# Pacing the bulk transfers of a fused decoder layer in counted TensorE time, and storing K and V once per pair of chunks

## The chip, the cores and the metric

The kernel runs on all eight cores of one Trainium2 chip. The metric is the device time of the slowest core in microseconds (us), as the median of several executions. Each execution lists the span and the mean granted TensorE clock of every core. The executions of this case show a second, slower state: in some of them all four cores of one die, sometimes of both, have a lower clock (0.80 to 0.96 as a mean), and the time is up to 14% longer (2957.6 us for the kernel before in the group of e13 to e16, where the median of its fast executions is 2599.1 us). Such executions were left out.

Two numbers are used side by side. The time is that of the slowest core. The mean span is the mean over the eight cores and all fast executions; it is less noisy, because the slowest of eight is a matter of luck as well as of work.

## The reference, cut to what matters

One decoder layer over 4 sequences of 8192 tokens, width 1024. It mixes a gated causal convolution and an attention with forgetting, then runs a dense gated feed-forward network.

```python
def reference(x, g_mix_pre, w_in, b_forget, conv_w, conv_b, conv_ln_g, conv_ln_b,
              w_out, g_mix_post, g_ffn_pre, w_gate, w_up, w_down, g_ffn_post):
    h = rmsnorm(x, g_mix_pre[l])
    proj = h @ w_in[l]                                       # 1024 -> 2568 columns
    a_val, a_gate, q, k, v, f_logit = jnp.split(proj, splits, axis=-1)
    u = a_val * jax.nn.sigmoid(a_gate)                       # gates
    u = causal_depthwise_conv(u, conv_w[l], conv_b[l])       # width 31, 512 channels
    conv_out = jax.nn.silu(layernorm(u, conv_ln_g[l], conv_ln_b[l]))
    ...                                                      # 8 heads of 64, causal softmax,
    attn = forgetting_attention(heads(q), heads(k), heads(v), log_f)   # logits + sum of log f
    mix = jnp.concatenate([conv_out, attn_out], axis=-1) @ w_out[l]
    x = x + rmsnorm(mix, g_mix_post[l])
    h = rmsnorm(x, g_ffn_pre[l])
    y = (jax.nn.silu(h @ w_gate[l]) * (h @ w_up[l])) @ w_down[l]       # 2816 wide
    return x + rmsnorm(y, g_ffn_post[l])
```

## The kernel before

Two cores share a sequence. Each computes K and V for all 16 chunks of 512 tokens, and queries, convolution, attention and feed-forward for its own 8 chunks (every other one). All engines follow one static order, recorded by a small scheduler when the program is built. A filler stream (first the projection stage, then the feed-forward stage) is interleaved with the attention stream by counted TensorE time: `fa[0]` is the counted time of filler matmuls so far, `fa[1]` that of attention. Counted means that the program adds 512/2400 us for 512 columns; nothing in it knows about waits. `tick()` runs deferred steps, one per so many filler groups, and `defer(tag, steps, first, every)` queues them. A buffer carries keys; a DMA or an instruction waits for whatever was recorded earlier on the same keys, including earlier readers.

Two queues carry the transfers. SP issues the ring loads of K and V that attention reads (136 KB each for K, five buffers), the loads of the feed-forward weights, and all stores. POOL issues x (four pieces of 512 KB per chunk), the windows u for the convolution (four pieces of 540 KB), and 60 conversions that read the float32 feed-forward weights and write bfloat16 copies (256 KB for one of the gate and up weights).

The parts that the change touches:

```python
    # weights of the gates, recorded before chunk 0's K and V; the "read" of hT[1] only sets its place in time
    wl("q", winQ, 0, C_Q, C_K, hT[0].keys[7:8])
    wl("g", winG, 0, 0, C_Q, hT[1].keys[7:8])
    yield from p_kv(0)
    yield from norm_fin(1)                 # writes hT[1]
    flush("h")
    load_x(2)
    ...
    # K and V, chunk i: one staging buffer for K, two for V, stores per chunk
    def st_k():
        for o in range(2):
            st("sp", k_s[:, 0:64, :].rearrange(...)[o, :, :, i * CH:(i + 1) * CH],
               kst[64 * o:64 * o + 64, :, :], kst.keys, [("k_s", i, o)], ("kst", o))
    defer("st", [st_k], 4)
    ...
    # x and u: deferred pieces
    defer("x", [lambda g=g: x_piece(nxt, g) for g in range(4)], 6, 2)
    defer("lu", [lambda s=s: ld("pool", u4, ...) for s in range(4)], 1, 3)
    ...
    # LayerNorm after the convolution: two temporaries, one step at every tick
    L, C = tmp[cb % 2], cvst[cb % 2]
    ...
    defer("ln", [fs[0][0], fs[1][0], fs[0][1], fs[1][1], fs[2][0], fs[0][2], fs[1][2],
                 fs[3][0], fs[2][1], fs[3][1], fs[2][2], fs[3][2]], 3)
    ...
    # last projection chunk: weights and activations of feed-forward block 0
    if last:
        ld("pool", wout, wout[:], wout_d)
        f_load(0)                          # conv and attention activations, 0.5 MB each, on SP
        f_loadx(0)                         # x1, 2 MB, on SP
    ...
    # the seam: first part of the feed-forward stream
    yield from conv_ln(J - 1)
    yield from A1(0, range(8))             # output projection of block 0, uses wout and the loads above
    yield from gates(J, 0, H)
    flush("ln")
    yield from A2(0)                       # norm and residual
    w_pump()
    for cb in (1, 2, 3):
        yield from gates(J, cb, H)
    yield from A3(0)
    ...
    # attention of block j starts 8 us of counted filler after its queries were queued for storing
    t0 = fa[0]
    while fa[0] < min(t0 + 8.0, p_end[0]):
        yield None
    ...
    # main loop
    for c in filler():
        fa[0] += c
        tick()
        ntick[0] += 1
        if cvt and ntick[0] > 90 and ntick[0] % 8 == 0:
            cvt_one()                      # one conversion on POOL
        ...                                # then attention steps, by a rate
```

The softmax here doesn't subtract the row's maximum and nothing guards it: scores larger than these inputs give would overflow.

## Time and profile before

The time before is 2597.2 us (median of 4 executions, 2587.4 to 2603.4). In the profiled execution the cores span 2560.4 to 2605.8 us with a mean of 2585.8 us. Core 6 was the slowest, and its page is shown first: the span, the busy time of each engine, and three of the rows of 40 slices (65 us each; tenths of busy time, of the granted clock and of the DMA engines).

```profile
span 2605.8 us, 53522 instructions; the slowest of 8 cores (2560.4 to 2605.8 us)
PE 2392.7 (92%) x19688; PEld 1216.8 (47%) x19688; DVE 993.7 (38%) x1506; ACT 1598.0 (61%) x1945; POOL 510.0 (20%) x835
PE   4887989899879978999999999999999999999996
PEclk8998989999999998999999999999999999999998
DMA  9656658596564744435544553653563564453443
```

TensorE is the limiter, but not evenly. From slice 17 on it is full. Up to about 1090 us it is not, and that is the projection stage and the seam to the feed-forward stage. The windows view of the same core gives the stages and, below, two windows of 16 us, a stall and what follows it. Columns: window, its length, busy time of PE, PEld, DVE, ACT and POOL with counts, granted clock, DMA share, GB/s.

```profile
0.00:65.00 65.00, 28.89 (x119) 9.77 (x119) 17.70 (x30) 13.43 (x21) 4.85 (x12) 0.88 0.95 180
65.00:330.00 265.00, 223.75 (x1748) 113.16 (x1749) 104.94 (x181) 137.09 (x193) 66.47 (x175) 0.91 0.62 146
330.00:600.00 270.00, 244.75 (x2296) 122.74 (x2294) 107.17 (x180) 177.41 (x220) 59.00 (x148) 0.97 0.67 148
600.00:892.00 292.00, 255.59 (x2397) 131.69 (x2396) 110.03 (x185) 182.84 (x223) 49.84 (x128) 0.95 0.62 135
1090.00:2366.00 1276.00, 1262.60 (x10711) 664.19 (x10709) 463.33 (x670) 908.35 (x1057) 241.02 (x270) 1.00 0.49 148
...
768.00:784.00 16.00, 2.82 (x21) 1.20 (x19) 1.38 (x2) 0.79 (x1) 0.00 (x0) 0.65 1.00 215
784.00:800.00 16.00, 16.00 (x155) 8.95 (x154) 3.94 (x7) 11.73 (x17) 3.38 (x15) 0.92 0.58 128
```

Between 768 and 784 us TensorE stood still for 13 us while the DMA share was 1.00; the clock in that window is 0.65 and still 0.92 in the next. What it waited for is in the view of waits, PE lines of core 6 (total us, times, longest), where `s_kr` is the K ring and `s_hT` the normalised chunk:

```profile
PE pbig L355 <- DMA s_kr_52<-k_s: 32.7, 4, 16.0
...
PE pbig L355 <- DVE s_hT_77 L438: 15.8, 4, 12.7
PE pbig L355 <- DMA s_kr_53<-k_s: 14.3, 3, 7.7
...
PE pbig L355 <- DMA s_kr_49<-k_s: 5.2, 1, 5.2
```

Two of these are seen in the chain of waits of core 6 (start, us, what). First the one long wait for `hT`, then the stall at 768 us:

```profile
30.42 33.96 DMA s_winG<-w_in
...
749.17 33.88 DMA s_kr_52<-k_s
```

At 30.42 us the load of the gate weights is issued; DVE may not write the last eighth of hT1 before it has landed, since that load is recorded as a reader of it. So part of these 34 us becomes a wait of TensorE, 12.7 us on core 6. At 749.17 us a ring load of 136 KB is issued and takes 34 us, while four pieces of x, four of u, four conversions and K and V stores are issued on core 6 (739 to 767 us; the DMA share from 739 to 784 us is 0.89); that these bytes delay it is what the experiments test.

| K-ring waits before, us per core | 0-190 us | about 205 us | 240-600 us | 600-850 us | seam, 850 us on | sum |
|---|---|---|---|---|---|---|
| before | 3.6 | 15.6 | 2.3 | 8.1 | 6.7 | 36.3 |

### The profile page before, as it was taken

What the parts mean: (1) busy time and instruction counts of PE and PEld (TensorE: products, weight loads), DVE (VectorE), ACT (ScalarE), POOL (GpSimd) and SP (SyncE); (2) the same over time, 40 slices, a digit from 0 to 9 for tenths busy, and PEclk for the clock granted to TensorE, in tenths of its full rate; (3) what the DMA queues carried; (4) which work ended last, traced back from release to release, by engine and by line L of the source; (5) the groups of instructions that cost most, each with busy time, mean ns of one, the idle gap of its engine ahead of it and who ended that gap; (6) DMA issues with size and microseconds to landing.
All of it is one profiled execution on the core that took longest, in us unless ns stands there. A gap on an engine that the chain in (4) does not pass through costs nothing.

```text
span 2605.8 us, 53522 instructions; the slowest of 8 cores (2560.4 to 2605.8 us)
## 1 busy us (share of the span) xinstructions
PE 2392.7 (92%) x19688; PEld 1216.8 (47%) x19688; DVE 993.7 (38%) x1506; ACT 1598.0 (61%) x1945; POOL 510.0 (20%) x835
## 2 busy tenths in 40 slices
PE   4887989899879978999999999999999999999996
PEld 1353434444344533455555555555555555554442
DVE  2442443434242344324424324424332342433643
ACT  2264766767566665777767767767767777773311
POOL 0141212121211122014013003102201401301401
PEclk8998989999999998999999999999999999999998
DMA  9656658596564744435544553653563564453443
GB/s 180 154 116 150 158 121 178 122 199 135 145 145 98 161 143 121 154 94 157 161 155 124 166 176 108 178 173 94 154 213 91 143 187 129 133 166 130 148 151 99
DMA packets 203468, 378.67 MB, mean 145 GB/s; under 512 B 23472, under 2 KB 117168, under 8 KB 201936
## 3 DMA queue, kind: packets, MB, share of 16 engines
q1 hardware_dynamic: 178608, 307.68, 40.6%
q0 software_dynamic: 24608, 67.56, 13.1%
q8 instruction: 166, 2.72, 0.4%
q14 instruction: 86, 0.70, 0.1%
HBM read 348.35 MB, written 68.81 MB: 160 GB/s over the span
## 4 chain that ended last, share of the span: by engine, by line
PE 72%; DMA 8%; ACT 8%; DVE 5%; issue 4%; SPq 1%; POOL 1%; DVEq 0%; ACTq 0%; POOLq 0%
PE pbig L355 72%; DMA s_kr_53<-k_s 3%; DMA s_kr_52<-k_s 2%; SPq L327 1%; DMA s_winG<-w_in 1%; ACT s_pt_61 L1004 1%; ACT s_pt_60 L1004 1%; ACT s_pt_59 L1004 1%; DMA q_s<-s_qst 1%; ACT L367 1%; DMA s_xs<-xT 1%; ACT s_sq L450 1%; POOL s_pt_61 L1009 1%; ACT s_pt_62 L1004 0%; ACT s_rstd L367 0%
## 5 line engine op out<-in xcount | busy, mean ns | idle before, releaser
L1004 ACT ACTIVATE s_pt_59<-pbig 128x1024 bf16<-128x1024 f32 x288 | 294.4, 1022 | 248.2 <-PE pbig L355 247.1
L1004 ACT ACTIVATE s_pt_60<-pbig 128x1024 bf16<-128x1024 f32 x288 | 294.3, 1022 | 145.1 <-PE pbig L355 143.5
L1004 ACT ACTIVATE s_pt_61<-pbig 128x1024 bf16<-128x1024 f32 x288 | 294.2, 1022 | 121.9 <-PE pbig L355 120.4
L1004 ACT ACTIVATE s_pt_62<-pbig 128x1024 bf16<-128x1024 f32 x224 | 228.9, 1022 | 82.8 <-PE pbig L355 80.9
L1009 POOL TENSOR_SCALAR_AFFINE_SELECT s_pt_61<-s_pt_61 128x128 bf16<-128x128 bf16 x192 | 67.5, 352 | 873.6 <-ACT s_pt_61 L1004 857.0
L844 DVE SCALAR_TENSOR_TENSOR s_sa_132<-s_th_93,pbig 128x512 f32<-128x512 f32 x88 | 60.4, 687 | 261.8 <-ACT s_th_93 L843 248.8
L844 DVE SCALAR_TENSOR_TENSOR s_sa_133<-s_th_94,pbig 128x512 f32<-128x512 f32 x88 | 60.4, 686 | 236.4 <-ACT s_th_94 L843 233.2
L392 POOL TENSOR_TENSOR s_ssA<-s_ssA,s_sqr_98 128x512 f32<-128x512 f32 x55 | 75.6, 1374 | 257.3 <-ACT s_sqr_98 L385 255.7
L355 PE MATMUL pbig<-s_h_123,s_wr_124 128*128 128x512 bf16 x464 | 121.4, 387 | 4.5 <-DVE s_h_123 L438 4.1
L392 POOL TENSOR_TENSOR s_ssA<-s_ssA,s_sqr_97 128x512 f32<-128x512 f32 x57 | 78.0, 1369 | 231.1 <-ACT s_sqr_97 L385 229.5
L355 PE MATMUL pbig<-s_h_123,s_wr_127 128*128 128x512 bf16 x480 | 122.1, 381 | 0.7 <-DVE s_sa_133 L844 0.7
L355 PE MATMUL pbig<-s_h_123,s_wr_125 128*128 128x512 bf16 x464 | 118.7, 381 | 3.3 <-DVE s_sa_133 L844 3.3
L355 PE MATMUL pbig<-s_h_123,s_wr_126 128*128 128x512 bf16 x480 | 121.2, 378 | 0.0
L355 PE MATMUL pbig<-s_h_123,s_wr_129 128*128 128x512 bf16 x464 | 117.4, 378 | 3.3 <-DVE s_sa_133 L844 1.8
L355 PE MATMUL pbig<-s_h_123,s_wr_128 128*128 128x512 bf16 x464 | 117.4, 378 | 0.0
L450 ACT ACTIVATE s_sq<-s_xs 128x512 bf16<-128x512 f32 x128 | 75.1, 625 | 50.1 <-DMA s_xs<-xT 49.8
L877 DVE COPY s_mix<-pbig 128x512 f32<-128x512 f32 x56 | 38.5, 688 | 153.1 <-PE pbig L355 153.1
L819 DVE COPY s_mix<-pbig 128x512 f32<-128x512 f32 x64 | 44.2, 691 | 105.5 <-PE pbig L355 105.5
L843 ACT ACTIVATE s_th_94<-pbig 128x512 f32<-128x512 f32 x88 | 52.2, 593 | 47.8 <-PE pbig L355 47.8
L355 PE MATMUL pbig<-s_sq,s_ones_bf 128*128 128x512 bf16 x192 | 56.2, 403 | 23.5 <-ACT s_sq L450 19.3
L355 PE MATMUL pbig<-s_u_84,s_w_82 128*32 128x512 bf16 x1024 | 70.4, 397 | 6.1 <-ACT s_th_94 L581 5.9
L843 ACT ACTIVATE s_th_93<-pbig 128x512 f32<-128x512 f32 x88 | 52.2, 594 | 36.0 <-PE pbig L355 30.9
(286 smaller groups left out, 4965.4 us busy)
## 6 DMA issues: line engine op xcount, KB each, us to landing
s_xs<-xT POOLq DMA_DIRECT2D x48, 512.0 KB, 8.2
s_u_84<-u_s POOLq DMA_DIRECT2D x32, 540.0 KB, 10.6
s_wr_126<-wg_b SPq DMA_DIRECT2D x30, 512.0 KB, 4.0
s_wr_127<-wu_b SPq DMA_DIRECT2D x30, 512.0 KB, 4.6
s_wr_124<-wg_b SPq DMA_DIRECT2D x29, 512.0 KB, 4.5
s_wr_125<-wu_b SPq DMA_DIRECT2D x29, 512.0 KB, 4.7
s_wr_128<-wg_b SPq DMA_DIRECT2D x29, 512.0 KB, 4.2
s_wr_129<-wu_b SPq DMA_DIRECT2D x29, 512.0 KB, 4.5
```

The source lines that it names most:

```text
L327: P.dma(q, lambda e: e.dma_start(out=out, in_=in_), reads=reads, writes=keys, sem=sem or buf.name)
L355: P.op("pe", lambda e: e.matmul(out, lhsT=lhsT, rhs=rhs, start=start, stop=stop, **kw), reads=reads, writes=[wkey])
L367: P.op("act", lambda e: e.activation(out=r[:, 0:ncol], in_=pb[b][:, 0:ncol], func=AF.Ln, bias=epsb[:, 0:1], scale=scale), reads=[PB(b)] + ...
L392: P.op(eng, lambda e: e.tensor_tensor(out=ss[:], in0=ss[:], in1=d[:], op=ALU.add), reads=ss.keys + d.keys, writes=ss.keys)
L450: defer("sq", [lambda k=k: P.op("act", lambda e: e.activation(out=sq[:, k, :], in_=xs[:, k, :], func=AF.Square), reads=[xs.keys[k]], write ...
L819: P.op("dve", lambda e, b=b, ob=ob: e.tensor_copy(out=mix[:, ob, :], in_=pb[b][:]), reads=[PB(b)], writes=[mix.keys[ob]])
L843: P.op("act", lambda e: e.activation(out=T[:], in_=pb[bg][:], func=AF.Tanh, scale=0.5), reads=[PB(bg)], writes=T.keys)
L844: defer("ff", [lambda: P.op("dve", lambda e: e.scalar_tensor_tensor(out=A[:], in0=T[:], scalar=1.0, in1=pb[bg][:], op0=ALU.add, op1=ALU.mult),
L877: P.op("dve", lambda e: e.tensor_copy(out=mix[:, ob, :], in_=pb[b][:]), reads=[PB(b)], writes=[mix.keys[ob]])
L1004: P.op("act", lambda e: e.activation(out=p[:], in_=pbig[:, 2 * s:2 * s + 2, :], func=AF.Exp), reads=[PB(2 * s), PB(2 * s + 1)], writes=p.keys)
L1009: sel = lambda e, ap: e.affine_select(out=ap, in_=ap, pattern=[[1, 128]], base=0, channel_multiplier=-1, compare_op=ALU.is_ge, fill=0.0)
```

## The change

Its intent: no two bulk transfers should leave POOL at once. x, u and the conversions pass through one list, one at a time, at least 3 us of counted TensorE time apart (conversions at least 10.5). K and V are staged for two chunks and stored once per pair, in rows twice as long. That needs room, which comes from sharing buffers; the LayerNorm gets by with one temporary and a slower pace, the gate weights load later, and the seam is put in another order. The core of the diff, with cuts marked:

```diff
-    kst = BP("kst", [128, 4, CH], BF16, parts=4)
+    kst = BP("kst", [128, 4, 2, CH], BF16, parts=8)
-    vst = [BP("vst0", [128, NH, 4, 65], BF16)]
...
+    vst = OV("vst", [128, NH, 8, 65], BF16, sqr[0])
...
+    bulk = []
+    def bulk_flush(tag):
+        for t in [t for t in bulk if t[0] == tag]:
+            bulk.remove(t)
+            t[1]()
...
-            defer("x", [lambda g=g: x_piece(nxt, g) for g in range(4)], 6, 2)
+            defer("x", [lambda g=g: bulk.append(("x", lambda: x_piece(nxt, g))) for g in range(4)], 6, 2)
...
-            L, C = tmp[cb % 2], cvst[cb % 2]
+            L, C = m2, cvst[cb % 2]
...
-        defer("ln", [fs[0][0], fs[1][0], fs[0][1], fs[1][1], fs[2][0], ...], 3)
+        defer("ln", [fs[0][0], fs[0][1], fs[1][0], fs[0][2], fs[1][1], ...], 3, 1 if j > NOWN - 3 else 2)
...
-        wl("g", winG, 0, 0, C_Q, hT[1].keys[7:8])
         yield from p_kv(0)
         yield from norm_fin(1)
         flush("h")
         load_x(2)
+        wl("g", winG, 0, 0, C_Q, hT[1].keys[7:8])
...
-        defer("lu", [lambda s=s: ld("pool", u4, ...) for s in range(4)], 1, 3)
+        for s in range(4):
+            bulk.append(("u", lambda s=s: ld("pool", u4, ...)))
...
-                   kst[64 * o:64 * o + 64, :, :], kst.keys, [("k_s", i, o)], ("kst", o))
-        defer("st", [st_k], 4)
+                   kst[64 * o:64 * o + 64, :, :, :].rearrange("p a b t -> p a (b t)"), kst.keys, [("k_s", j, o)], ("kst", o))
+        if own:
+            defer("st", [st_k], 4)
...
+            while not cvt_done.issuperset(keys):      # in w_pump: a conversion that is needed is forced
+                cvt_one()
...
+        yield from A1(0, range(8))
         yield from conv_ln(J - 1)
-        yield from A1(0, range(8))
-        yield from gates(J, 0, H)
-        flush("ln")
         yield from A2(0)
         w_pump()
-        for cb in (1, 2, 3):
+        for cb in range(4):
             yield from gates(J, cb, H)
         yield from A3(0)
+        yield ("att", 4.0)                            # 4 us of attention
...
-        if cvt and ntick[0] > 90 and ntick[0] % 8 == 0:
+        t = fa[0] + fa[1]
+        if bulk and t >= nb[0]:
+            nb[0] = t + 3.0
+            bulk.pop(0)[1]()
+        elif cvt and t >= nb[0] and t >= nb[1]:
+            nb[0], nb[1] = t + 3.0, t + 10.5
             cvt_one()
```

## The prediction

> **What bounds the kernel now.** One static instruction order per core, with TensorE the limiter. The windows of the slowest core (core 6, 2605.8 us) show two regimes. From 1090 to 2366 us TensorE is busy 1262.6 of 1276 us at clock 1.00: nothing to gain. From 0 to 1090 us it is busy 923 us at clock 0.88 to 0.97: 167 us idle, and roughly 60 us lost to the lower clock. That is the projection stage and its seam with the feed-forward stage; the change touches only these.
>
> What TensorE waits for there (table of waits, core 6): K-ring loads 52 us in 8 waits (longest 16.0); one DVE write of hT 12.7 us; squares 19 us; exponentials, tanh and attention normalisation some 60 us in pieces of 1 to 3 us. K-ring waits are about 15 us on core 1 (2560 us), 26 on core 0, 39 and 45 on cores 2 and 3: most of the spread between cores. They coincide with DMA shares of 0.9 to 1.07 over 15 to 45 us. At 738 to 784 us x (2 MB), u (2.1 MB), five conversions and two sets of K/V stores pass together; K-ring loads then take 11 to 34 us in the chain of waits. [...]
>
> **What the change does.**
> 1. x, u and conversions leave POOL one at a time, 3 us of counted TensorE work apart, conversions 10.5. In the built order only about 38 of 60 conversions remain in the projection stage; the rest move into the first feed-forward block, where the DMA share is about 0.5. For the 738 us burst I count about 7 MB for 10.
> 2. K/V per pair: 16 K stores for 32, 8 V stores for 16, rows twice as long, same bytes. Nothing is ready later: readiness was per pair already. With 1: three quarters of the K-ring waits go: -35 us on the slowest cores, -10 on the fastest.
> 3. The gate weights load after hT1 is written. Before, their load (34 us) "read" hT1's last eighth, so DVE could not write it until the load landed: -12 us (8.5 to 15 on other cores).
> 4. LayerNorm steps every 2 ticks instead of 1: same work, less bunched against exponentials: -5 us.
> 5. Seam: A1 before the LayerNorm statistics, gates undivided, 4 us of attention before the first feed-forward matmul. Waits of 4.7, 4.1, 2.5 and several of 1 to 2 us stand at 908 to 1000 us: -10 us.
> 6. Each removed long stall removes a stretch at lower clock: windows of 16 us after stalls show 0.76 to 0.92, about 3 us each: -12 us. [...]
>
> Added: no matmuls; the 1 MB V store can still hold K loads behind it.
>
> **Prediction.** 2596.5 - 76 = 2520 us; range 2485 to 2560. Faster by over 2%: 0.74; within 2%: 0.24; slower: 0.02.
>
> **What would show it.** TensorE waits on K-ring loads below 15 us on every core; no 12 us wait at 52 us, chunk 2's matmuls starting near 73 us instead of 87; DMA share rarely 1.0 from 330 to 890 us; V stores of 1040 KB landing within 20 us; clock from 65 to 890 us up from 0.91-0.97 to 0.96 or more; the part after 1090 us unchanged in length; cores within 30 us of each other.
>
> **What would make it wrong.** x, u and K/V bytes alone still fill the DMA engines; larger stores delay ring loads; the winG load competes with x(2) and returns the 12 us; small ACT-bound gaps keep the clock low.

## More of the kernel before

K-ring waits, with all buffers of the ring counted, were 52.2 us on core 6 and 21.9 us on core 1.

Before, core 6 had issued all 60 conversions when the last chunk's first K copy came.

## The result, and the profile after

The changed kernel takes 2566.4 us (median of 4 executions, 2563.2 to 2572.5), against 2597.2 us. The ratio is 0.9887, with a 95% interval of 0.9851 to 0.9924; in a later group of runs it was 0.9836 (0.9794 to 0.9877; run `e5_changed_again`, on chip 12). A ratio is the mean time of one kernel's fast runs over that of the other's of the same rounds, so it is not quite the ratio of the medians. The gain is real, 31 us, and less than 2% in the first comparison. The prediction, 2520 us with 2485 to 2560, was too low by 46 us and its range missed.

The page of the slowest core after (core 0):

```profile
span 2570.9 us, 53213 instructions; the slowest of 8 cores (2547.3 to 2570.9 us)
PE 2378.1 (92%) x19358; PEld 1219.1 (47%) x19688; DVE 993.2 (39%) x1505; ACT 1604.7 (62%) x1951; POOL 510.0 (20%) x835
PE   6887899999899779999999999999999999999895
PEclk9998999999999889999999999999999999999997
DMA  8764656467375755765635645554563563444542
```

(330 PE records are missing from this trace, 19358 against 19688, so small differences in PE busy time are not read.) The cores now lie within 24 us of each other instead of 45. The first slice is fuller (6 tenths for 4), and the dip moved (core 6 before and core 0 after, so only roughly comparable): before, slices 12 and 15 had 7 tenths, now slices 14 and 15 have (about 835 to 965 us), with a clock of 0.8 there. The stages of core 6, for comparison with the windows above:

```profile
0.00:65.00 65.00, 40.53 (x166) 14.83 (x170) 21.92 (x35) 18.03 (x29) 4.88 (x12) 0.95 0.82 164
65.00:330.00 265.00, 222.25 (x1755) 114.39 (x1784) 105.96 (x183) 140.44 (x194) 64.09 (x172) 0.92 0.62 148
330.00:600.00 270.00, 254.06 (x2441) 130.76 (x2469) 119.67 (x203) 198.94 (x247) 56.26 (x138) 0.99 0.64 146
600.00:892.00 292.00, 261.13 (x2493) 134.75 (x2526) 100.02 (x168) 186.59 (x224) 56.50 (x152) 0.95 0.68 147
1090.00:2366.00 1276.00, 1250.87 (x10339) 659.92 (x10530) 468.13 (x675) 887.04 (x1038) 246.08 (x276) 1.00 0.51 149
```

The first 65 us hold 12 us more work, the stretch from 330 us 9 us more. From 65 to 330 us nothing changed, and the clock from 600 to 892 us is 0.95 as before. The K-ring waits of core 6 in the view of waits fell from 52.2 us in eight waits to 28.1 us in five:

```profile
PE pbig L355 <- DMA s_kr_53<-k_s: 15.5, 1, 15.5
...
PE pbig L355 <- DMA s_kr_52<-k_s: 6.2, 1, 6.2
...
PE pbig L355 <- DMA s_kr_50<-k_s: 3.4, 2, 2.7
...
PE pbig L355 <- DMA s_kr_49<-k_s: 3.0, 1, 3.0
```

On core 1, the fastest before, they rose from 21.9 to 24.1 us, each time in three waits. The two longest are at the same places on every core: one at about 205 us, one at the seam. The chain of waits of core 6 shows the second one, and the 8 us windows what it costs:

```profile
842.73 35.48 DMA s_kr_53<-k_s
```

```profile
848.00:856.00 8.00, 8.00 (x111) 3.55 (x109) 1.44 (x2) 4.80 (x6) 1.37 (x5) 1.00 0.95 166
856.00:864.00 8.00, 6.96 (x110) 2.86 (x102) 2.25 (x3) 4.78 (x7) 3.01 (x10) 1.00 1.00 202
864.00:872.00 8.00, 0.00 (x0) 0.00 (x0) 0.00 (x0) 0.56 (x1) 1.12 (x2) 0.55 0.99 264
872.00:880.00 8.00, 1.32 (x3) 0.57 (x5) 0.00 (x0) 0.44 (x1) 0.00 (x0) 0.50 0.72 199
```

A ring load issued at 842.73 us lands at 878.2 us, TensorE stands from 863 to 878 us, and the clock falls to 0.50. The profile before has 0.92 in the 16 us from 784 us on, which is an estimated 2.6 us at half clock (16 times 0.08, doubled). The clock record itself has 0.50 from 864.7 to 881.8 us, where TensorE stood from 863.0 to 878.5; before, it has 0.50 until 786.6 us, 3.3 us after the stall. What that clock costs is in the timeline before: four matmuls of 512 columns took 1.91 us from 784.1 us on, at 0.50, and 1.03 us from 788.3 us on, at 1.00.

What that ring load stands behind is in the timeline, the queue of SP first and then POOL's issues, core 6 (start, us of issuing, what):

```profile
838.20 0.37 SPq L330 DMA_DIRECT2D v_s<-s_vst  x1
838.62 0.58 SPq L327 DMA_DIRECT2D s_cv<-conv_s  x1
839.25 2.24 SPq L327 DMA_DIRECT2D s_at<-attn_s  x1
841.52 0.79 SPq L327 DMA_DIRECT2D s_x_0_117<-xT  x1
...
842.73 0.44 SPq L327 DMA_DIRECT2D s_kr_53<-k_s  x1
...
844.48 16.32 SPq L327 DMA_DIRECT2D s_kr_49<-k_s  x1
```

```profile
839.26 0.59 POOL L327 DMA_DIRECT2D s_wout<-w_out  x1 [5.66 <-PE pbig L355]
839.84 0.53 POOL L430 DMA_DIRECT2D wg_b<-w_gate  x1
847.13 0.55 POOL L430 DMA_DIRECT2D wu_b<-w_up  x1 [0.22 <-issue]
864.52 0.60 POOL L430 DMA_DIRECT2D wu_b<-w_up  x1
```

Within 5 us there leave a V store (1 MB), the activations of block 0 (twice 0.5 MB), x1 (2 MB), the output weights (2 MB written) and a conversion, then the ring load, then another conversion. The next ring load after it needs 16 us to be issued at all.

To say where time went on all eight cores, stretches were cut at fixed pieces of work: the first K copy to SBUF of chunks 1, 2, 4, 8, 12, 14 and 15, the second and the last load of convolution activations in the feed-forward stage, and the end. Means over the eight cores of the profiled execution, us; the last five columns are the K-ring waits of TensorE:

| kernel | to chunk 1 | 1-2 | 2-4 | 4-8 | 8-12 | 12-14 | 14-15 | seam | steady | tail | span | 0-190 | at 205 | 240-600 | 600-850 | seam wait |
|---|---|---|---|---|---|---|---|---|---|---|---|---|---|---|---|---|
| before | 65.3 | 23.9 | 159.3 | 239.8 | 226.0 | 113.3 | 22.0 | 221.4 | 1275.4 | 239.4 | 2585.8 | 3.6 | 15.6 | 2.3 | 8.1 | 6.7 |
| changed | 53.5 | 25.7 | 151.9 | 233.7 | 218.3 | 108.0 | 24.1 | 224.2 | 1275.3 | 244.5 | 2559.3 | 1.6 | 7.7 | 0.0 | 0.0 | 15.2 |

So 11.8 us come from the start and 24.7 us from the stretches between chunks 1 and 14. The stretch into chunk 15, the seam and the tail took 10.0 us back. Half of what the tail lost is an accident of this execution: see the last section. Waits for K-ring loads fell by 11.8 us per core, not by 35: the stalls from 240 to 850 us are gone, the one at 205 us was halved, and that of the seam more than doubled.

### The profile page after: what moved, and what is told of

Same layout as the page of the kernel before. It is cut to its first block, busy times and chain, and to the rows that moved or that the text cites. A ratio compares the mean times of both kernels' runs of the same rounds, so it can differ in the third digit from the quotient of the medians.

```text
span 2570.9 us, 53213 instructions; the slowest of 8 cores (2547.3 to 2570.9 us)
## 1 busy us (share of the span) xinstructions
PE 2378.1 (92%) x19358; PEld 1219.1 (47%) x19688; DVE 993.2 (39%) x1505; ACT 1604.7 (62%) x1951; POOL 510.0 (20%) x835
## 3 DMA queue, kind: packets, MB, share of 16 engines
q1 hardware_dynamic: 165936, 307.68, 41.3%
## 4 chain that ended last, share of the span: by engine, by line
PE 77%; ACT 8%; DMA 4%; DVE 4%; issue 4%; POOL 1%; SPq 1%; DVEq 0%; ACTq 0%; POOLq 0%
PE pbig L355 77%; ACT s_pt_60 L1018 1%; ACT s_pt_61 L1018 1%; ACT s_pt_59 L1018 1%; DMA s_kr_53<-k_s 1%; SPq L327 1%; DMA k_s<-s_kst 1%; DMA q_s<-s_qst 1%; ACT s_sq L461 1%; ACT L367 1%; DMA s_xs<-xT 1%; ACT s_pt_62 L1018 1%; DMA s_kr_50<-k_s 1%; POOL s_pt_61 L1023 0%; ACT s_rstd L367 0%
## 5 line engine op out<-in xcount | busy, mean ns | idle before, releaser
L355 PE MATMUL pbig<-s_h_121,s_wr_123 128*128 128x512 bf16 x452 | 118.4, 387 | 4.1 <-DVE s_sa_131 L859 3.4
L355 PE MATMUL pbig<-s_h_121,s_wr_124 128*128 128x512 bf16 x455 | 119.5, 385 | 1.5 <-DVE s_sa_131 L859 0.2
L355 PE MATMUL pbig<-s_h_121,s_wr_125 128*128 128x512 bf16 x459 | 118.4, 381 | 1.8 <-DVE s_sa_131 L859 0.7
L355 PE MATMUL pbig<-s_h_121,s_wr_127 128*128 128x512 bf16 x435 | 111.9, 378 | 4.9 <-DVE s_sa_131 L859 1.8
L355 PE MATMUL pbig<-s_h_121,s_wr_122 128*128 128x512 bf16 x434 | 114.2, 387 | 2.0 <-issue 0.4
L355 PE MATMUL pbig<-s_h_121,s_wr_126 128*128 128x512 bf16 x448 | 114.9, 378 | 0.9
L461 ACT ACTIVATE s_sq<-s_xs 128x512 bf16<-128x512 f32 x128 | 75.0, 625 | 50.5 <-DMA s_xs<-xT 50.1
L858 ACT ACTIVATE s_th_93<-pbig 128x512 f32<-128x512 f32 x88 | 52.2, 593 | 52.6 <-PE pbig L355 52.6
L858 ACT ACTIVATE s_th_92<-pbig 128x512 f32<-128x512 f32 x88 | 52.2, 593 | 38.8 <-PE pbig L355 33.7
## 6 DMA issues: line engine op xcount, KB each, us to landing
s_u_83<-u_s POOLq DMA_DIRECT2D x32, 540.0 KB, 11.8
```

The lines of the kernel that those rows point to most:

```text
L355: P.op("pe", lambda e: e.matmul(out, lhsT=lhsT, rhs=rhs, start=start, stop=stop, **kw), reads=reads, writes=[wkey])
L461: defer("sq", [lambda k=k: P.op("act", lambda e: e.activation(out=sq[:, k, :], in_=xs[:, k, :], func=AF.Square), reads=[xs.keys[k]], write ...
L858: P.op("act", lambda e: e.activation(out=T[:], in_=pb[bg][:], func=AF.Tanh, scale=0.5), reads=[PB(bg)], writes=T.keys)
```

## The experiments

Eighteen runs were made, in five groups, each group on one chip with the kernel before. The table has, from the fast runs, the median time of the slowest core, its ratio with the 95% interval, and the mean span less that of the kernel before on the same chip. This last difference repeats within about 2 us in the one pair that tests it (runs `e6` and `e18` are the same kernel: -41.3 and -39.8). But the kernel before itself differs by 3 us between two groups on one chip (2588.5 and 2585.3 us of mean span on chip 12; 2590.9 and 2587.7 on chip 5), so less than 3 us between runs of different groups is not read as an effect.

| run | median us | ratio | mean span less before, us |
|---|---|---|---|
| e1_gate_load_alone | 2585.9 | 0.9957 (0.9910-1.0004) | -12.6 |
| e2_no_conv_in_seam | 2561.8 | 0.9848 (0.9826-0.9870) | -31.9 |
| e3_store_per_chunk | 2567.8 | 0.9871 (0.9849-0.9893) | -27.1 |
| e4_old_seam | 2565.5 | 0.9862 (0.9840-0.9884) | -26.5 |
| e5_changed_again | 2565.6 | 0.9836 (0.9794-0.9877) | -31.4 |
| e6_early_loads_and_hold | 2557.4 | 0.9808 (0.9766-0.9850) | -41.3 |
| e7_spacing_undone | 2573.2 | 0.9859 (0.9816-0.9902) | -27.0 |
| e8_spaced_all_conversions | 2573.5 | 0.9862 (0.9821-0.9904) | -23.4 |
| e9_ln_every_tick | 2595.1 | 0.9949 (0.9932-0.9966) | -4.1 |
| e10_pairs_only | 2604.8 | 0.9979 (0.9955-1.0004) | -0.3 |
| e11_spacing_only | 2596.2 | 0.9952 (0.9936-0.9969) | -2.1 |
| e12_best | 2558.4 | 0.9803 (0.9781-0.9826) | -42.9 |
| e13_old_ln_in_changed (wrong result) | 2573.0 | 0.9905 (0.9891-0.9919) | -19.3 |
| e14_pairs_only_old_ln | 2584.7 | 0.9948 (0.9920-0.9975) | -11.9 |
| e15_spacing_only_old_ln | 2574.5 | 0.9908 (0.9891-0.9925) | -17.5 |
| e16_new_ln_only | 2584.4 | 0.9950 (0.9933-0.9966) | -11.4 |
| e17_block1_later | 2544.6 | 0.9768 (0.9734-0.9801) | -51.8 |
| e18_early_loads_again | 2558.4 | 0.9817 (0.9785-0.9848) | -39.8 |

The stretches, as in the table above:

| kernel | to chunk 1 | 2-4 | 4-8 | 8-12 | 12-14 | 14-15 | seam | steady | at 205 | 240-850 | seam wait | waits for ACT |
|---|---|---|---|---|---|---|---|---|---|---|---|---|
| before | 65.3 | 159.3 | 239.8 | 226.0 | 113.3 | 22.0 | 221.4 | 1275.4 | 15.6 | 10.4 | 6.7 | 47.0 |
| e1 | 52.8 | 159.8 | 238.7 | 224.1 | 109.1 | 21.8 | 222.0 | 1275.4 | 16.6 | 6.2 | 7.3 | 45.4 |
| e2 | 52.8 | 152.9 | 233.2 | 218.3 | 107.8 | 23.0 | 218.0 | 1277.1 | 8.1 | 0.0 | 7.5 | 44.9 |
| e3 | 52.7 | 150.2 | 232.9 | 218.8 | 108.0 | 27.8 | 220.3 | 1276.3 | 7.8 | 0.3 | 12.7 | 45.4 |
| e4 | 52.8 | 152.1 | 233.6 | 218.3 | 108.0 | 23.6 | 226.5 | 1276.2 | 7.5 | 0.0 | 14.6 | 43.6 |
| e5 (changed) | 53.7 | 152.8 | 233.3 | 218.0 | 107.7 | 23.7 | 224.5 | 1275.5 | 8.7 | 0.0 | 15.3 | 45.4 |
| e6 | 53.1 | 151.8 | 232.0 | 217.3 | 107.7 | 22.9 | 215.0 | 1277.3 | 8.0 | 0.0 | 0.0 | 49.2 |
| e7 | 53.4 | 163.8 | 235.3 | 218.8 | 109.0 | 23.3 | 216.4 | 1275.2 | 16.4 | 2.3 | 6.7 | 45.5 |
| e8 | 53.7 | 151.9 | 232.3 | 217.8 | 108.1 | 25.9 | 230.0 | 1275.2 | 8.5 | 0.2 | 21.8 | 45.3 |
| e9 | 53.2 | 152.1 | 240.4 | 225.9 | 114.1 | 26.6 | 229.7 | 1275.5 | 8.2 | 0.0 | 15.5 | 60.0 |
| e13 | 53.5 | 153.0 | 235.5 | 219.5 | 108.0 | 25.8 | 226.8 | 1275.4 | 8.2 | 0.0 | 14.4 | 50.5 |
| e14 | 53.5 | 166.6 | 234.7 | 220.0 | 109.8 | 27.0 | 220.5 | 1275.6 | 17.5 | 1.2 | 6.1 | 45.1 |
| e15 | 53.4 | 152.6 | 236.8 | 219.6 | 107.6 | 26.7 | 229.5 | 1274.9 | 8.3 | 0.3 | 14.6 | 46.3 |
| e16 | 53.2 | 161.2 | 236.6 | 229.6 | 111.2 | 21.5 | 220.5 | 1275.5 | 16.4 | 13.1 | 6.7 | 43.9 |
| e18 (e6 again) | 53.5 | 151.8 | 233.4 | 218.5 | 108.2 | 22.8 | 214.8 | 1277.8 | 8.8 | 0.0 | 0.0 | 49.6 |
| e17 | 53.2 | 139.4 | 228.5 | 218.3 | 110.6 | 20.3 | 213.9 | 1286.1 | 3.9 | 0.5 | 0.0 | 54.1 |

(The stretches of e5 and e8 up to the seam are from seven cores, since a landmark was missing on the eighth. "Waits for ACT" is what TensorE waited for ACT from 30 to 1120 us. Chunks 1 to 2 took 25.5 to 27.2 us in every variant and are left out.)

The theory after the first look: the change works in the middle of the projection stage, and the delayed conversions, now in the seam, give part of it back; the rest of the seam's wait is x1 and the activations. The rivals: the new order of the seam is what costs; or the doubled V store is, by holding ring loads behind it; or the conversions do not matter, and the seam's loads alone fill the engines.

### e1: the gate weights' load alone

```diff
 # the kernel before, with one line moved
-        wl("g", winG, 0, 0, C_Q, hT[1].keys[7:8])
         ...
         load_x(2)
+        wl("g", winG, 0, 0, C_Q, hT[1].keys[7:8])
```

> The kernel before with one line moved: the gate weights load after hT1 is written. Theory: the start-up gain of 9 to 13 us seen on the changed kernel is this line's alone, so chunk 2's first K copy comes at 77 to 82 us (86 to 93 before) and the whole run is 8 to 12 us shorter than before (ratio 0.9955 to 0.997). Rival: the later load only competes with chunk 2's input or with later traffic, and less than 4 us is left at the end.

Measured: -12.6 us of mean span, chunk 1 reached at 52.8 us instead of 65.3. The stall at 205 us and that of the seam are as before. This one line is worth some 12 of the change's 31 us. One of the six executions (2619.5 us) had two cores at a clock of 0.958; without it the difference is -15.4 us. By stretches, about 2 of the 12.5 us won up to chunk 1 are lost again from chunk 1 to 2 (26.1 us instead of 23.9).

### e2: no conversions in the seam

```diff
 # the changed kernel
+        if last:
+            hold[0] = True                  # from the K of the last chunk ...
-        elif cvt and t >= nb[0] and t >= nb[1]:
-            nb[0], nb[1] = t + 3.0, t + 10.5
+        elif cvt and t >= nb[0] and t >= nb[1] and not hold[0]:
+            nb[0], nb[1] = t + 3.0, t + pace[0]
         yield ("att", 4.0)
+        hold[0], pace[0] = False, 8.0       # ... to the end of the seam
```

> The changed kernel, but no weight conversion is issued from the last chunk's K projection to the first feed-forward matmul (they follow at 8 instead of 10.5 us of counted work). Theory A: the new K-ring stall of 14.4 to 16.7 us that every core shows at about 857 to 872 us comes from conversions that the change moved there; it falls to 6 us or less, and the run is 10 to 14 us faster than the changed kernel (about 2553 us). Theory B (the doubled V and K stores hold the ring load) and theory C (w_out, x1, the two activations are a burst of their own, the old kernel only met it less exposed): the stall stays at 11 us or more and the time within 5 us of the changed kernel.

Measured: the seam's wait fell from 15.2 to 7.5 us per core, the seam from 224 to 218 us. So the few conversions in it cause about half of the wait. The end gained at most 4 to 5 us (slowest core 2561.8); by mean span, -31.9 against -31.4 (e5, another group), nothing. The steady part became 1.6 us longer. On core 6 the 24 conversions that were left went out in bunches between 935 and 1149 us, up to four within 2 us; that this made the steady part longer is likely and not shown.

### e3: stores per chunk again, spacing kept

```diff
 # the changed kernel
-                   kst[64 * o:64 * o + 64, :, :, :].rearrange("p a b t -> p a (b t)"), kst.keys, [("k_s", j, o)], ("kst", o))
-        if own:
-            defer("st", [st_k], 4)
+                   kst[64 * o:64 * o + 64, :, i % 2, :], kst.keys[i % 2::2], [("k_s", i, o)], ("kst", o))
+        defer("st", [st_k], 4)
 # and the same for V, from one half of the pair's buffer
```

> The changed kernel, but K and V are stored per chunk again, in rows half as long, from the same buffers. Theory B: the stall at 857 to 872 us shrinks by 5 us or more and nothing else gets worse: 5 to 10 us faster than the changed kernel. Rival (the long rows are what removed the K-ring stalls of chunks 11 to 15): stalls of 5 us or more come back on some cores between 600 and 830 us, and the run is 10 to 25 us slower than the changed kernel. If the even spacing of loads removed them, neither happens: within 5 us, with the stall at 12 to 16 us.

Measured: -27.1 us, against -31.4 us for the changed kernel (e5, on another chip). No stall came back between 240 and 850 us (0.3 us), the seam's wait is 12.7 us. With the spacing in place the longer stores add nothing that these runs can tell from zero: at most 4 us. With stores per chunk the seam's wait is 2.5 us shorter than in e5 (12.7 against 15.3 us), so the doubled store may be that much of it while conversions pass beside it. Without conversions there it adds nothing: e7 and e14 below have the doubled store and waits of 6.7 and 6.1 us, as before the change (6.7). The second rival falls for the most part.

### e4: the old order of the seam

```diff
 # the changed kernel, with the seam as before
+        yield from conv_ln(J - 1)
         yield from A1(0, range(8))
-        yield from conv_ln(J - 1)
+        yield from gates(J, 0, H)
+        flush("ln")
         yield from A2(0)
...
-        yield ("att", 4.0)
```

> The changed kernel with the order of the seam as before (LayerNorm statistics first, gates split, no attention ahead of the first feed-forward matmul). If the new order is worth the 10 us that I predicted, this run is 8 to 12 us slower than the changed kernel. The traces say less: from the end of the K-ring stall to the second load of conv activations the new order is 4 us shorter on core 1, so 2 to 6 us slower is what I now expect, with the stall at 860 us unchanged at 14 to 17 us.

Measured: the seam takes 226.5 us instead of 224.3, the wait in it is 14.6 us. By this stretch the new order is worth 2 to 3 us (by mean span -26.5 against -31.4 us, but in different groups), and it does not cause the stall. The first rival falls.

### e5: the changed kernel again, as a reference on the chip of the next three

> The changed kernel once more, unaltered, to have it on the same chip as the next three. Expected: ratio to before 0.985 to 0.989, mean span of the eight cores 2554 to 2558 us, one K-ring stall of 14 to 17 us at about 870 us on every core.

Measured: 2565.6 us, ratio 0.9836, and the same stretches as in the first profile within 1 us, except the tail (242.5 us instead of 244.5). Two of its six executions were slow.

### e6: block 0's activations loaded one chunk earlier, and no conversions in the seam

```diff
 # e2, with the conversions resumed at a pace of 5.5 instead of 8.0, and
         if last:
             ld("pool", wout, wout[:], wout_d)
-            f_load(0)
-            f_loadx(0)
...
+        if i == NCH - 2:                    # during chunk 14
+            f_loadx(0)
+            f_load(0)
```

> The changed kernel with no conversion in the seam (as in e2_no_conv_in_seam, resumed at 5.5 us of counted work so that none is forced later), and with x1, the conv activations and the attention output of the first own chunk loaded during chunk 14 instead of in the seam (3 MB out of the burst). Theory: the seam stall is bytes ahead of the ring load; conversions were 8 us of 15 and the remaining 5.8 to 9.7 us of e2_no_conv_in_seam fall below 3: mean span 2544 to 2548 us, ratio 0.980 to 0.983. Rival: what is left is the K and V stores of the last pair and w_out, and the stall stays at 5 us or more with a mean above 2551.

Measured: the seam's wait is 0.0 us on every core, the mean span -41.3 us, 10 us better than the changed kernel on the same chip. The windows of core 6 in the place of the stall (shown above for the changed kernel):

```profile
856.00:864.00 8.00, 7.94 (x77) 4.43 (x76) 2.00 (x5) 5.88 (x9) 2.50 (x6) 1.00 0.25 70
864.00:872.00 8.00, 7.95 (x68) 4.17 (x67) 3.34 (x6) 6.31 (x8) 3.80 (x4) 1.00 0.17 52
```

TensorE is full at clock 1.00, with a DMA share of 0.17 to 0.25 where it was 0.99. The stall is thus made of conversions (half, e2) and of the loads of x1 and the activations (the other half). The loads stood there before the change already; the conversions were put there by it.

### e7: spacing undone

```diff
 # the changed kernel: x, u and conversions leave as before
-            defer("x", [lambda g=g: bulk.append(("x", lambda: x_piece(nxt, g))) for g in range(4)], 6, 2)
+            defer("x", [lambda g=g: x_piece(nxt, g) for g in range(4)], 6, 2)
 # the same for u
-        elif cvt and t >= nb[0] and t >= nb[1]:
+        ntick[0] += 1
+        if cvt and ntick[0] > 90 and ntick[0] % 8 == 0:
```

> The changed kernel with only the bulk queue undone: x, u and conversions leave POOL as before (all conversions by 645 us of counted work); pairs, seam, LayerNorm and gate load stay changed. Theory: the bulk queue is the whole of the change beyond the gate load, so K-ring stalls of 3 to 13 us come back on most cores near 640 to 660 and 770 to 790 us, the stall at about 210 us grows to 14 to 18, the seam stall falls to 4 to 10, and the mean span is 2566 to 2573 us, as for e1_gate_load_alone. Rival: pairs, seam and LayerNorm do part of it together, mean 2560 or less.

Measured: -27.0 us, 4.4 us worse than the changed kernel on the same chip. Without spacing, the stretch from chunk 2 to 4 is 11 us longer (the wait at 205 us is back at 16.4 us), but the seam is 8 us shorter (216.4 us, wait 6.7 us), since its conversions are done by then. And between 240 and 850 us the stalls stay away: 2.3 us against 10.4 before. So the spacing, the headline of the change, is worth 11 us from chunk 2 to 4 and 4 us from there to chunk 14, and costs 8 us at the seam.

### e8: conversions at a pace of 6.0, so that more are done before the seam

```diff
-            nb[0], nb[1] = t + 3.0, t + 10.5
+            nb[0], nb[1] = t + 3.0, t + 6.0
```

> The changed kernel with conversions at 6 instead of 10.5 us of counted work, still through the one queue: about 50 instead of 36 of 60 before the last chunk, so nearly the bytes of before in the projection stage, but spaced. If fewer bytes (conversions moved out) cured the K-ring stalls of chunks 11 to 15, stalls of 3 us or more come back there on several cores and the mean is 6 us or more above the changed kernel. If the even distance cured them, none comes back, and the mean is within 3 us of the changed kernel (the seam keeps its conversions).

Measured: -23.4 us. The seam's wait grew to 21.8 us and the seam to 230 us. Fewer conversions are left for it (9 instead of 14), but five instead of three leave in its first 60 us, where the stall stands. It is not how many conversions are left that counts, but how many pass while the seam's loads do. Taken with e2 (7.5 us with none) and the changed kernel (15.2 us with three) the wait follows the number of conversions there.

### e9: LayerNorm at every tick

```diff
-  ..., 3, 1 if j > NOWN - 3 else 2)
+  ..., 3, 1)
```

> The changed kernel with the LayerNorm steps at every tick again, as before. I predicted the spreading to be worth 5 us. TensorE's waits on ACT after the start-up were 47.0 us a core before and 44.7 after, so what I expect now is a mean span within 2 us of the changed kernel (2557) and the same lengths of the stretches between chunks 4, 8 and 12 (233 and 218 us). If it is 4 us or more slower there, the spreading is what shortened them.

Measured: -4.1 us, so this one number costs 27 us. It is a mixture that neither kernel has: one temporary, but a step at every tick. The waits of TensorE for ACT grow from 45 to 60 us per core. That is half of it. The other part is in the clock records: the time that TensorE is busy at a clock of 0.50 grows from 89.7 us (e5) to 111.3 us per core, an estimated 11 us of work at full clock (half of the difference). The view of waits, core 1, has it in the exponentials of attention; first the changed kernel (`e5`), then this one:

```profile
PE pbig L355 <- ACT s_pt L1018: 29.7, 28, 3.3
```

```profile
PE pbig L355 <- ACT s_pt L1018: 40.5, 30, 3.3
```

With a single temporary, the tanh of one quarter cannot start before DVE has read that of the quarter before, and the exponentials recorded behind it on ACT wait too; this part is read from the program, the waits are measured (29.7 and 40.5 us). The slower pace is the price of the single temporary, not a gain by itself.

### e10 and e11: pairs alone, spacing alone, with that LayerNorm

```diff
 # e10: the changed kernel with spacing undone (e7), the old seam (e4) and LayerNorm at every tick (e9)
 # e11: the changed kernel with stores per chunk (e3), the old seam (e4) and LayerNorm at every tick (e9)
```

> The kernel before with the gate load moved and K and V stored per pair, nothing else (bulk transfers as before, seam order and LayerNorm pace as before; the order of the LayerNorm steps is that of one temporary). e7_spacing_undone kept nearly the whole gain from chunk 4 to 14 without spacing, and e3_store_per_chunk kept it without pairs. Theory: pairs and spacing each suffice against the K-ring stalls of chunks 4 to 15. Then here the stalls from 240 to 850 us sum to 3 us or less a core, stretches 4-8 and 8-12 take 233 to 236 and 217 to 220 us, and the mean is 2560 to 2566. Rival: LayerNorm pace did it, and the stretches are as in e1_gate_load_alone (239 and 224 us), mean 2570 or more.

> The kernel before with the gate load moved and the one bulk queue, nothing else (K and V per chunk, old seam, LayerNorm every tick). Theory: spacing alone too clears the K-ring stalls from 240 to 850 us (3 us or less a core) and halves the one at about 205 us to 6 to 9 us, but pays with 12 to 16 us at the seam: mean 2557 to 2563. Rival: without pairs the spacing does not suffice, stalls of 5 us or more near 640 and 780 us on several cores, mean above 2566.

Measured: -0.3 and -2.1 us. These runs were badly designed. They were meant to have "the rest as before", but took the LayerNorm of e9, which neither kernel has, and its 27 us bury what was to be seen. Read without e9 they would have said that neither part of the change is worth anything. e14 and e15 repeat them with the LayerNorm that the kernel before really had.

### e12: the first u window later

```diff
 # e6, with the load of u for block 0 queued after the store of the second queries
-        load_u(0)
         yield from p_own(3)
...
+        if i == 3:
+            load_u(0)
```

> e6_early_loads_and_hold, and the first conv window (2.1 MB) is queued after the second Q store instead of before it. On the changed kernel the Q store that the attention of the second block waits for took 14 us to land, behind three window pieces that left POOL back to back although counted 3 us apart, because POOL had waited for a store. Theory: with the window behind it the Q store lands in 8 us or less, the stall at about 205 us falls from 8 to 4 us or less on most cores, mean 2540 to 2545. Rival: the store waits for bytes whichever transfer they belong to, and the stall stays at 7 us or more; mean within 2 us of e6_early_loads_and_hold (2547).

Measured: -42.9 us, within the noise of e6, and the wait at 205 us is unchanged (9.2 us, against 8.0 to 8.8 us). But the run did not test what it was made for. In its trace the four pieces of u still left POOL just before the query stores: at 181.0 to 182.9 us, with the stores issued at 185.0 and 185.6 us (core 6; core 1 the same within 2 us). The stores then took 12.2 and 13.1 us to land. So the 2.1 MB were not out of the way, and whether the wait is made by u stays open. Three of its six executions were slow; the fast ones took 2554.4 to 2559.9 us. The name was premature.

### e13: the old LayerNorm in the changed kernel (wrong result)

```diff
-            L, C = m2, cvst[cb % 2]
+            L, C = tmp[cb % 2], cvst[cb % 2]
-        defer("ln", [fs[0][0], fs[0][1], fs[1][0], ...], 3, 1 if j > NOWN - 3 else 2)
+        defer("ln", [fs[0][0], fs[1][0], fs[0][1], ...], 3)
```

> The changed kernel with the LayerNorm of before, complete: two temporaries, old order, a step every tick. If the LayerNorm's pace is worth what I predicted (5 us), mean span 2560 to 2564. If it is behind the stretches between chunks 4, 8 and 12 (233 and 218 us against 239 and 224 to 226 before), these go back to 238 and 223 or more and the mean is 2568 to 2576. If the pace only repays what the one temporary costs, the mean is within 3 us of the changed kernel (2557).

Measured: -19.3 us, with a wrong result (relative error 0.174). Read from the program: in the new order of the seam the residual step of A2 is recorded between LayerNorm steps and overwrites `tmp`. The work and the order are the same, so the time can be compared, but no more than that. Two things follow. The new seam and a LayerNorm in the two `tmp` buffers do not go together as they are. And the new LayerNorm as a whole is worth 7 to 12 us in the changed kernel (12 by the table, -31.4 against -19.3, in two groups on the same chip; 7 by the profiled executions, 2565.9 against 2558.6 us).

### e14, e15, e16: one part at a time, with the old LayerNorm

```diff
 # e14: the kernel before + the gate load moved + K and V per pair
 # e15: the kernel before + the gate load moved + the spacing
 # e16: the kernel before + the gate load moved + the new LayerNorm
```

> Gate load moved and K and V stored per pair, all else as before, now with the old LayerNorm complete. If K-ring stalls were the matter and pairs suffice: stalls from 240 to 850 us sum to 3 us or less a core and the stretches 4-8 and 8-12 are 235 and 219 us, mean 2561 to 2566. If the LayerNorm's pace was: 238 and 223 us, mean 2567 to 2573, hardly better than e1_gate_load_alone.

> Gate load moved and the one bulk queue, all else as before, with the old LayerNorm complete. If spacing suffices against the stalls and these were the matter: stretches 2-4, 4-8, 8-12 of 152, 233 and 219 us, seam stall 11 to 16 us, mean 2557 to 2562. If the LayerNorm's pace was: 152, 238 and 223 us, mean 2564 to 2570.

> Gate load moved and the new LayerNorm (one temporary, a step every second tick), all else as before. If the pace was the matter: stretches 4-8 and 8-12 of 234 and 219 us apart from K-ring stalls, waits on ACT below 45 us a core, mean 2560 to 2565. If not: as e1_gate_load_alone, 239 and 224 us, mean 2569 to 2575.

Measured: -11.9, -17.5 and -11.4 us, where the gate load alone gives -12.6 us (e1). So pairs alone are worth nothing, the new LayerNorm alone nothing, and the spacing alone 5 us (2 us, if e1 is read without its odd execution). Yet pairs and spacing both do what they were made for: between 240 and 850 us the K-ring waits are 1.2 and 0.3 us instead of 10.4 (6.2 in e1). Pairs lose it again from chunk 2 to 4 (166.6 us against 159.8 us in e1, the wait at 205 us being 17.5 us) and into chunk 15 (27.0 against 21.8 us), the spacing at the seam (229.5 us against 222.0). They are two remedies for one stall, and together do not remove it twice. And the new LayerNorm pays only once these stalls are gone: in e16 the stalls are still there (13.1 us). That ACT catches up during them is the likely reason, argued and not shown.

### e17 and e18: attention of blocks 0 and 1 later

```diff
 # e18 is e6 again, as a control. e17 is e6 with
-            while fa[0] < min(t0 + 8.0, p_end[0]):
+            while fa[0] < min(t0 + {0: 11.0, 1: 15.0}.get(j, 8.0), p_end[0]):
```

Why: the wait at 205 us had withstood every experiment. The chain of waits of core 6 in the changed kernel shows it as a store of queries, then a ring load behind it:

```profile
191.84 10.21 DMA q_s<-s_qst
...
202.49 5.85 DMA s_kr_52<-k_s
```

Attention of block 1 starts so early that its own queries are still being stored. If that is so, more filler before it must help, whatever else is in flight. The edit delays block 0 too (11 us of filler instead of 8), so the two are not told apart.

> e6_early_loads_and_hold with the attention of the first two blocks starting 11 and 15 us of counted work after their Q is ready, instead of 8. Theory: the stall near 205 us (6.8 to 9.7 us a core, and 7 to 11 in e12_best) is attention standing too early in the static order behind its own Q store: it falls below 2 us, and with the clock after it the mean span falls by 6 to 11 us against e18_early_loads_again. Rival: the wait only moves, because the later start makes attention denser afterwards and the exponentials bound it: mean within 3 us.

> e6_early_loads_and_hold unaltered, as control: mean span 2545 to 2549 us, ratio to before 0.979 to 0.983, stall near 205 us of 7 to 10 us a core, none at the seam.

Measured: e17 takes 2544.6 us (2542.3 to 2550.3), ratio 0.9768; its result is correct. Against e18 on the same chip the mean span is 12.0 us lower. The wait at 205 us fell to 3.9 us, the stretch from chunk 2 to 4 from 151.8 to 139.4 us. Of 18.6 us gained up to the end of the seam, the steady part took back 8.3 us (1286.1 us against 1277.8): presumably the attention that was not done early is done there. e17 is faster than both kernels. The shorter wait alone does not explain the gain, though: it is 5 us less, and the idle time of TensorE over the whole run did not fall (165.6 us in e18, 166.5 us in e17, mean of the cores). What fell is the time that TensorE is busy at a clock of 0.50, from 93.7 us per core (90.0 in e6, the same kernel as e18) to 72.2 us, an estimated 11 us of work at full clock (half of the difference). Nearly all of it is between chunks 4 and 15 and in the seam, after the wait at 205 us. Why the later start has this effect there no run shows.

## Why the prediction was wrong, point by point

It predicted -76 us (its six terms add up to -74); -31 us came. Term by term, the size predicted and what the runs show of it:

| term of the sum | predicted | shown |
|---|---|---|
| K-ring waits | -35 slowest cores, -10 fastest | -11.8 mean (36.3 to 24.5); -24 on core 6, the slowest; +2 on core 1, the fastest |
| gate weights' load | -12 | -11.8 up to chunk 1, -10.0 up to chunk 2 (first profile); -12.6 of the whole (e1) |
| LayerNorm pace | -5 | 0 alone (e16), -7 to -12 in the changed kernel (e13) |
| seam | -10 | -2 to -3 for the order (e4), +2.8 for the whole stretch |
| clock | -12 | an estimated -3: TensorE is busy at a clock of 0.50 for 91.5 us per core instead of 96.7; half of the difference |

**The step that failed** is point 2, "three quarters of the K-ring waits go: -35 us on the slowest cores, -10 on the fastest". One third went. Three errors were in it.

- *Three stalls were taken for one.* The prediction looked at the burst at 738 us and put all K-ring waits down to it. By place, only 10.4 of the 36.3 us stood between 240 and 850 us, and these did go to 0.0. The 15.6 us at about 205 us were only halved. The spacing did that (16.4 us without it, e7; 8.3 us with it alone, e15). In the rest a query store just ahead of its attention has a part: e17 more than halves it with a later start (8.8 to 3.9 us). Whether the pieces of u that leave just before that store make the other part is open, since e12 did not move them.
- *What was moved was not followed to where it went.* The prediction counted that 22 conversions leave the projection stage and says they go "into the first feed-forward block, where the DMA share is about 0.5". On the way there they cross the seam, where the block's own loads pass. The wait there rose from 6.7 to 15.2 us on the mean. e2 (7.5 us without conversions), e8 (21.8 us with more) and e7 (6.7 us with conversions done early) show that the conversions did this; e6 (0.0 us) shows that the loads of x1 and activations are the rest.
- *The slowest core's waits were added to a median.* Core 6 had 52 us of them, the mean core 36. A slowest core of a profiled execution has had bad luck in part, and that is not to be gained twice. What the spread gave is the difference between slowest and mean, from 16 us (2601.4 less 2585.1 us, on the chip of e1) to 11 us (2566.3 less 2555.2 us): 5 us.

**The gate weights' load** was right in mechanism and nearly in size. Chunk 2's first K copy came at 79.2 us instead of 89.2, so of the 11.8 us won up to chunk 1 about 2 were lost again before chunk 2; the worry that the later load competes with x(2) may be that part.

**The clock term** fell with the first: the seam's stall, with its clock of 0.50, moved into the last stage as others left it. That the clock is lower in a stall was seen again (0.50 in the stall; 1.00 in e6 where there is none), the sum was not: with a third of the K-ring waits gone, TensorE's busy time at 0.50 fell by 5 us of 97 (mean of the cores), little more than one kernel differs from itself (90.0 us in e6, 93.7 in e18). Most of it thus stands elsewhere than at these stalls: between chunks 4 and 8, where the change left no K-ring wait, it is 20.8 us before and 21.8 after.

**The seam term** was mis-sized: -2 to -3 us for the new order, not -10. With the conversions out of the way (e7: 216.4 us against 222.0 in e1) the stretch gains 5 to 6 us.

**The LayerNorm term** was too small in the changed kernel and is nothing alone. The reason given, "less bunched against exponentials", is half of it: e9 shows that the pace mends first of all what the single temporary breaks.

**Of the signs** named: V stores of 1040 KB land in 16.3 us (median; named: within 20), the part after the seam is unchanged (1275.4 and 1275.3 us), the cores lie within 24 us (named: 30). K-ring waits are below 15 us on no core (20.7 to 29.1 us; named: below 15 on every core), the clock reached 0.96 only from 330 to 600 us (0.92, 0.99, 0.95), and a DMA share of 0.95 or more was hardly rarer from 330 to 890 us (3 to 6 of 35 windows of 16 us per core, 4 to 7 before). **Of the worries** named, the larger stores cost little: at most 4 us of time and some 2.5 us of the seam's wait (e3). That small gaps keep the clock low fits the clock records: in the changed kernel, core 6 has seven of 0.50, of 3.4 or 6.8 us each, between 240 and 850 us, where no K-ring wait stands. Six follow idle gaps of TensorE of 1.7 to 2.9 us, one several of up to 1.1 us; ACT ended five of these waits and DVE two. No run tests it alone.

What stays open: why the stretch from chunk 2 to 4 gets longer with pairs alone (166.6 us against 159.8), and why the tail is 3 us longer in the changed kernel (242.5 us in e5 against 239.4 before). In the first profiled execution it was 5 us longer on the mean, because cores 0 and 1 had 253.8 and 249.8 us at a lower clock (stretches of 0.81, last section). What makes the wait at 205 us, beyond the early start, is open too.

## What to carry to other kernels

Before adding up what a change removes, list the stalls of all cores by their place in time, and give each its own cause; a total by name of the buffer that is waited for mixes several. When a change delays transfers, look up in the built order what they will then run beside, for here some 10 us of the gain waited at a stage boundary (e6 against the changed kernel). Two remedies for the same stall are worth one, and a slack that stalls had hidden may be worth something only after they are gone (here ACT's, argued and not shown). And look in the trace whether an experiment moved what it was to move: e12 did not, and looked like an answer.

## What the traces say of the clock and of transfers, and leave open

- In one slow execution of the kernel before (group of e1) the cores of one die have 0.803 to 0.807 and 2943 to 2949 us, those of the other die 0.97 and 2569 to 2590 us. In the fast profiled executions every core ran dense matmuls for 1276 us (before the change TensorE was busy 1251 to 1263 us of it) at a granted clock of 1.00. But each trace counts time from its own core's first instruction, so it does not show how many cores of a die did this at once. What decides between the two states no run here shows.
- Whether the cores of a die ran together no trace shows directly. The profile of the changed kernel has a hint. The clock records of all four cores of die 0, and of none of die 1, have four stretches of 0.81, of 14.5, 13.3, 16.9 and 14.7 us (one end cut off on two cores). They begin at 2453 us on cores 0 and 1, but at 34 us on cores 2 and 3. The windows view shows the first two on core 0 and then on core 2:

```profile
2454.00:2466.00 12.00, 11.91 (x46) 4.99 (x46) 3.79 (x6) 1.79 (x3) 0.00 (x0) 0.81 0.43 149
...
2480.00:2491.00 11.00, 10.91 (x42) 4.57 (x42) 3.43 (x5) 1.56 (x3) 0.00 (x0) 0.81 0.24 70
...
36.00:48.00 12.00, 12.00 (x76) 5.49 (x75) 3.66 (x6) 2.34 (x5) 0.00 (x0) 0.81 0.61 92
...
62.00:73.00 11.00, 11.00 (x67) 4.89 (x65) 3.77 (x6) 1.15 (x2) 0.00 (x0) 0.81 1.03 170
```

  If these are the same four events, cores 2 and 3 started an estimated 2418 us after cores 0 and 1 (from the starts of the stretches), and the lower clock fell where all four ran. It is a reading of one trace, not tested.
- Twice the bytes landed in about the same time: of the V stores of core 6, 520 KB took 20.6 and 14.8 us (medians of the two buffers before), 1040 KB took 16.3 us after. But e14 shows what such batching is worth when the store is not on the critical path: nothing (-11.9 us, of which the moved gate load is -12.6 us).
- Spacing issues in a counted order does not space them in time. In the changed kernel, on core 1, three pieces of u that were 3 us of counted time apart left within 2 us, because POOL had been held up by a wait of 5.3 us ahead of them. The timeline (start, us, what):

```profile
177.74 0.75 POOL L327 DMA_DIRECT2D s_u_83<-u_s  x1 [5.29 <-ACT s_sq L461]
179.95 1.95 POOL L327 DMA_DIRECT2D s_u_83<-u_s  x3
```
